# HGRN2 levels of 2 and 4 tokens, and of 8 and 16, computed as two groups of products

## The chip, the cores and the metric

The kernel runs on one core of one Trainium2 chip. The metric is the device time of one execution in microseconds, the median of three runs. TensorE (PE in the profile) does the matrix products, VectorE (DVE), ScalarE (ACT) and GpSimd (POOL) the rest, and SyncE (SP) issues the loads.

## The reference

Two layers of a block with three token mixers side by side (retention, HGRN2, differential attention) and a convolutional feed-forward part, for 16 meta tokens and 256 tokens of width 1024 in float32. What the change touches is the score matrix of HGRN2. For each of 8 heads of 128 features it is, between a query and an earlier key, the sum over features of query times key times the product of the forget gates between them:

```python
def step(state, xs):
    qc, kc, vc, lfc = xs
    cb = jnp.cumsum(lfc, axis=1)
    rel = cb[:, :, None] - cb[:, None, :]
    dec = jnp.where(causal, jnp.exp(jnp.where(causal, rel, 0.0)), 0.0)
    a = jnp.einsum('bqhd,bkhd,bqkhd->bhqk', qc, kc, dec)
    o = jnp.einsum('bhqk,bkhe->bqhe', a, vc) + jnp.einsum('bqhd,bhde->bqhe', qc * jnp.exp(cb), state)
```

The decay has a feature axis, so `a` is no single matrix product.

## The kernel before

**The main stream.** All weights are cut into 128x128 tiles, loaded in chunks of eight (`wraw`), split into a high half (`whi`, by ACT) and the rest (`wlo`, by DVE), and multiplied with the activations in three products each (lines 862 to 864, tile `main`). These products follow each other on TensorE from the first microsecond to the last; a pair of weight columns takes 48 of them, and `ORDER` (line 58) sets the order of the pairs. Everything else, the three mixers included, is put between them.

**The planner.** `_Plan` collects every operation with a cost, a due time (`key`) and its tiles, and writes out one fixed order for each engine. Names in `ORDER` that begin with `+`, `!` or `*` are marks: `+hgb` puts the scores of the second group of HGRN2 heads into the plan, and `!hgb` says by when they are due, since the due times of a part are spread up to the clock at its mark. All calls of ACT, DVE and small products go through one helper, line 549, so the profile gives them that line.

**The scores of HGRN2** (`hg_heads`, line 1010). It is called for two groups of four heads in each of two layers, four calls in all. The decay is split by reach: `LEVELS` are 1, 2, 4, 8, 16, 32 and 64. At reach s a token block of 2s has a left half of keys and a right half of queries. The keys `k` (`hf` in the profile) hold the decay up to the end of their half, the queries `q` (`hq`) that from the start of theirs, so one product gives the scores between the two halves. Afterwards the queries of the right half are multiplied by the total of the left half, the keys of the left half by the total of the right half, and the totals (`total`, tile `tot`) are multiplied in pairs.

For reach 1 to 16 the scores of four heads, two chunks and four blocks of 32 tokens are 32 small products (`quarters`, line 1057): the stationary side is the keys of one block of 32 tokens, the moving side the queries that are wanted, and four such products lie beside each other in four column strips of the array. The result is a bank `lev` of PSUM, from which masked copies (`fill`, line 1042, COPY_PREDICATED by DVE, with masks from `lev` of `masks`) write the wanted entries into `near`, 8 blocks of 32 columns. Reach 1 lists all 32 queries. Reach 2 lists 16 queries of its right halves and, from `odd` in the scratch tile `extra`, 16 odd queries that belong to reach 1. Reach 4, 8 and 16 list 16 queries each. Reach 32 and 64 (lines 1090 to 1122) go straight to the matrix `at`.

The 16 tokens behind the 256 (the tail) are handled by themselves: their keys and queries of each reach are copied by ACT into `kt` and `qt` (`qt1`, `qt2`, `qt4`, `qt8`), multiplied in two products `pm` and copied under masks into `am`. The products `px` (line 1163) connect the first chunk with the second one.

**Buffers.** `extra` has one of 14 slots of 4 times 272 columns. The gates (`hg`, `rg`, `m0`, `m1`, `m2`) have three buffers of 8 times 272 columns.

Of the kernel before, what the change touches and what calls it, by code (L numbers as in the profile page):

```python
# [13 lines left out]
U8 = mybir.dt.uint8  # L14
# [5 lines left out]
P = 128  # L20
# [3 lines left out]
T = META + SEQ  # L24
# [7 lines left out]
DA_DH = 64  # L32
MASKED = -1e30
LEVELS = (64, 32, 16, 8, 4, 2, 1)
TAIL = T - 2 * P
BANK = 512
CHUNK_TILES = 8
# [14 lines left out]
def _pairs(name, lo, hi):  # L52
    return [(name, j) for j in range(lo, hi)]
# [170 lines left out]
def _constants():  # L224
    f = np.float32
    c = np.zeros((P, C_END), f)
    c[:, C_COS_R : C_COS_R + T], c[:, C_SIN_R : C_SIN_R + T] = _rope_tables(RET_DK, 1)
    c[:, C_COS_D : C_COS_D + T], c[:, C_SIN_D : C_SIN_D + T] = _rope_tables(DA_DH, 2)
    k = np.arange(P)
    c[:, C_MASK + T - P : C_MASK + T] = np.where(k[None, :] <= k[:, None], 0.0, MASKED)  # L230
    c[:, C_IDENT : C_IDENT + P] = np.eye(P, dtype=f)
    lg = np.log1p(-np.exp2(-5.0 - np.arange(RET_HEADS, dtype=f))).astype(f)
    def decay(keys, queries):
        gap = (queries[None, :] - keys[:, None]).astype(f)
        d = np.exp(lg[None, :, None] * np.maximum(gap, 0)[:, None, :]) * f(RET_DK ** -0.5)
# [12 lines left out]
    c[:, C_FIRST:C_SUM] = np.where((hd == to) & (key <= q), 0.0, MASKED)  # L248
    c[:, C_SUM:C_MAP] = (hd == to) & (key == q)
    c[:, C_MAP:] = np.concatenate([m == 0, m == 1], axis=1)  # L250

    def level(s, keys, queries):
        q, key = np.arange(queries)[None, :], np.arange(keys)[:, None]
        return ((key // (2 * s) == q // s) & (key % (2 * s) < s)).astype(f)

    def odd(keys, queries):
# [7 lines left out]
    lev[:, :112] = np.tile(np.concatenate(block, axis=1), (4, 1))  # L266

    inner = [even(TAIL, 16), level(2, TAIL, 8), odd(TAIL, 8), level(4, TAIL, 8), level(8, TAIL, 8)]
    lev[:64, 2 * 64 :] = np.concatenate([np.kron(np.eye(4, dtype=f), x) for x in inner], axis=1)
    return c, dec, lev  # L270


# [335 lines left out]
def _trace(ctx, tc, plan, a, depth, probe):  # L608
# [41 lines left out]
    def bank(name):  # L650
        return new(bp, [P, 512], F32, "bank", 2, name)
# [4 lines left out]
    def tt(out, x, y, op):  # L656
        dve.tensor_tensor(out=out, in0=x, in1=y, op=op)
# [29 lines left out]
    masks = fixed([P, 5 * 64], "masks", U8)  # L687
    lev = masks[:, : 2 * 64]
    inner = masks[:64, 2 * 64 :]
    lev_f = slot("levf")[:, : 5 * 64]  # L690
    sync.dma_start(lev_f, a["lev"])
    plan.key = 18.0 + EARLY
    dve.tensor_copy(masks, lev_f)
# [243 lines left out]
    for li in range(depth):  # L937
# [72 lines left out]
        def hg_heads(b):  # L1010
# [28 lines left out]
            def right(t, s):  # L1039
                return halves(t, s, t.shape[2])[:, :, :, 1, :]  # L1040

            def fill(out, mask, x):

                s = out.shape[3]
                mask = mask.rearrange("p (n s) -> p n s", s=s).unsqueeze(1).to_broadcast([P, 8, 16 // s, s])
                dve.copy_predicated(out, mask, x.rearrange("p g (n s) -> p g n s", s=s))

            def blocks(calls, out, *moving):


# [15 lines left out]
            act.activation(odd[:, :, :, 64:], q[:, :, : 2 * P].rearrange("p h (c n two) -> p h c n two", c=2, two=2)[:, :, :, :, 1], AF.Copy)  # L1066
            tt(right(q, 1), right(q, 1), right(total, 1), MUL)
            room, at0 = slot("tot"), 0
            for i, s in reversed(list(enumerate(LEVELS))):

                pl = bank("lev")
                wide = pl[:, :256].rearrange("p (g t) -> p g t", g=8)
                some = pl[:, :128].rearrange("p (g t) -> p g t", g=8)
                tokens = lambda c, t: slice(c * P + 32 * t, c * P + 32 * t + 32)
                if s == 1:
                    quarters(wide, q, lambda hd, c, t: q[:, hd, tokens(c, t)])
                    dve.copy_predicated(near, lev[:, 80:112].unsqueeze(1).to_broadcast([P, 8, 32]), wide)
                elif s == 2:  # L1080
                    act.activation(odd[:, :, :, :64].rearrange("p h c (n s) -> p h c n s", s=2),
                                   q[:, :, : 2 * P].rearrange("p h (c n two s) -> p h c n two s", c=2, two=2, s=2)[:, :, :, :, 1, :], AF.Copy)
                    quarters(wide.rearrange("p g (two t) -> p g two t", two=2), odd,
                             lambda hd, c, t: odd[:, hd, c, :].rearrange("p (two t) -> p two t", two=2)[:, :, 16 * t : 16 * t + 16])
                    fill(right(near, 2), lev[:, 48:64], wide[:, :, :16])
                    fill(right(near, 1), lev[:, 64:80], wide[:, :, 16:])
                elif s < 32:
                    quarters(some.rearrange("p g (n s) -> p g n s", s=s), q, lambda hd, c, t: right(q[:, hd : hd + 1, tokens(c, t)], s)[:, 0])
                    fill(right(near, s), lev[:, 16 * (i - 2) : 16 * (i - 1)], some)
                elif s == 32:  # L1090
                    for t in range(4):
                        here = slice(32 * t, 32 * t + 32)
# [14 lines left out]
                else:  # L1107
# [15 lines left out]
                if s <= 8:  # L1123
                    act.activation(kt[:, 6 - i, :, :], k[:, :, tail], AF.Copy)
                    if s == 1:
                        act.activation(qt1, q[:, :, tail], AF.Copy)
                    else:
                        to = {2: qt2[:, :, :8], 4: qt4, 8: qt8}[s]
                        act.activation(to.rearrange("p h (n s) -> p h n s", s=s), right(q[:, :, tail], s), AF.Copy)

                end = 2 * P if s > 8 else T
                n = end // (2 * s)
                both = total[:, :, : 2 * n].rearrange("p h (n two) -> p h n two", two=2)
                first = both[:, :, :, 0:1]
# [6 lines left out]
                kl = halves(k, s, end)[:, :, :, 0, :]  # L1141
                tt(kl, kl, both[:, :, :, 1:2].to_broadcast([P, 4, n, s]), MUL)
                total = room[:, at0 : at0 + 4 * n].rearrange("p (h n) -> p h n", h=4)
                at0 += 4 * n
                tt(total.unsqueeze(3), first, both[:, :, :, 1:2], MUL)
# [426 lines left out]
```

## Time and profile before

| | before |
|---|---|
| time, median of 3 runs | 1330.01 us (1329.83 to 1330.66) |
| time of the profiled execution | 1330.22 us |
| its span, first to last instruction | 1328.4 us |
| granted TensorE clock | 0.999 |
| DMA, mean over the span | 164 GB/s |

The span is what the views of the profile cover; the time also holds what lies around it. In a row of a timeline the first number is the start in microseconds from the start of the span, the second the duration, then come engine, line, operation, output and inputs, shapes and count; rows that follow each other with the same text are merged. A duration overlaps the next instruction of the same engine, so what an instruction costs its engine is read from one start to the next. In the rows of `lev` the three numbers behind the colon are the least, median and greatest duration in nanoseconds. In rows by stretch each engine has its busy time and, in brackets, its instructions. A float32 product on TensorE stands as two records.

### The profile page before, as it was taken

The page shows a single profiled execution, that of the slowest core. Times are in us where ns is not written, and L with a number is a line of the kernel's source. Part 1 is how long each engine was busy: PE and PEld are TensorE (multiplying, and loading weights), DVE is VectorE, ACT ScalarE, POOL GpSimd, SP SyncE. Part 2 cuts the span into 40 slices and gives each one's busy share as a digit, 9 for nine tenths or more (in the row PEclk, how much of TensorE's full clock was granted, in tenths as well). Part 3 has the DMA queues.
Part 4 walks back from the last instruction along what each step waited for, and adds up shares of the span by engine and source line. Part 5 has one row for each costly group of instructions (what it writes and reads, how often), then busy time and mean ns, then how long its engine had stood idle before and what let it go on. Part 6 is the DMA issues. An engine that isn't in the chain of part 4 may idle for free.

```text
span 1328.4 us, 28916 instructions
## 1 busy us (share of the span) xinstructions
PE 1317.2 (99%) x11862; PEld 1288.8 (97%) x11862; DVE 962.0 (72%) x1630; ACT 813.3 (61%) x1372; POOL 83.6 (6%) x161
## 2 busy tenths in 40 slices
PE   9999999999999999999999999999999999999998
PEld 9999999999999999999999999999999999999986
DVE  7575777697576689886564757776985867898753
ACT  6747454746676567665446474557565775766643
POOL 5000000001010020000030000000011100200000
PEclk9999999999999999999999999999999999999999
DMA  7644543443544545555555445444445445465653
GB/s 270 193 142 153 167 161 128 143 143 128 179 139 159 175 159 175 182 170 187 177 173 179 158 157 163 160 136 144 141 153 175 141 160 198 138 208 189 199 184 109
DMA packets 60755, 219.07 MB, mean 165 GB/s; under 512 B 6864, under 2 KB 6992, under 8 KB 60624
## 3 DMA queue, kind: packets, MB, share of 16 engines
q1 hardware_dynamic: 60336, 216.71, 49.6%
q8 instruction: 93, 1.52, 0.5%
q10 hardware_dynamic: 288, 0.52, 0.1%
q14 instruction: 38, 0.31, 0.1%
HBM read 216.16 MB, written 1.05 MB: 164 GB/s over the span
## 4 chain that ended last, share of the span: by engine, by line
PE 94%; DVE 4%; issue 1%; ACT 0%; DMA 0%; SPq 0%; DVEq 0%
PE main L862 27%; PE main L864 27%; PE main L863 26%; PE fo L1372 2%; PE fo L1374 2%; PE fo L1373 2%; PE lev L1053 1%; DVE two_b L549 1%; PE ds L1237 1%; DVE wlo L549 1%; PE ms L549 1%; PE do L549 1%; PE ro L549 1%; PE ho L549 1%; PE vt L549 1%
## 5 line engine op out<-in xcount | busy, mean ns | idle before, releaser
L862 PE MATMUL main<-xh,whi 128*128 128x272 f32 (+1 forms) x2368 | 693.4, 293 | 0.3 <-issue 0.3
L864 PE MATMUL main<-xh,wlo 128*128 128x272 f32 (+1 forms) x2368 | 680.4, 287 | 0.7 <-DVE wlo L549 0.6
L863 PE MATMUL main<-xl,whi 128*128 128x272 f32 (+1 forms) x2368 | 671.7, 284 | 2.8 <-DVE xl L549 2.8
L549 DVE TENSOR_TENSOR wlo<-wraw,whi 128x1024 fp32r<-128x1024 f32 (+1 forms) x408 | 496.8, 1223 | 201.2 <-ACT whi L549 200.3
L549 ACT ACTIVATE whi<-wraw 128x1024 fp32r<-128x1024 f32 (+1 forms) x408 | 426.5, 1048 | 231.5 <-PE main L863 166.1
L863 PEld LDWEIGHTS main<-xl,whi 128*128 128x128 f32 x2368 | 448.9, 190 | 4.0 <-DVE xl L549 3.4
L862 PEld LDWEIGHTS main<-xh,whi 128*128 128x128 f32 x2368 | 445.6, 188 | 2.1 <-issue 0.4
L864 PEld LDWEIGHTS main<-xh,wlo 128*128 128x128 f32 x2368 | 444.6, 188 | 2.0 <-DVE wlo L549 2.0
L549 DVE SCALAR_TENSOR_TENSOR two_b<-main,small,two_b 128x256 f32<-128x256 f32 (+2 forms) x144 | 65.4, 487 | 29.1 <-ACT two_b L549 27.4
L549 ACT ACTIVATE two_b<-main,small 128x272 f32<-128x272 f32 (+1 forms) x72 | 37.3, 566 | 28.7 <-PE main L864 28.7
L549 POOL TENSOR_TENSOR y<-h,rstd 128x272 f32<-128x272 f32 x32 | 34.8, 1121 | 316.4 <-ACT rstd L549 316.4
L864 PE MATMUL main<-ghi,wlo 128*128 128x272 f32 x176 | 51.0, 290 | 0.0
L862 PE MATMUL main<-ghi,whi 128*128 128x272 f32 x176 | 50.9, 289 | 0.0
L863 PE MATMUL main<-glo,whi 128*128 128x272 f32 x176 | 50.2, 285 | 0.0
L549 ACT ACTIVATE vsrc<-main 128x544 f32<-128x544 f32 x24 | 15.0, 626 | 39.4 <-PE main L864 39.2
L862 PE MATMUL main<-b0hi,whi 128*128 128x272 f32 (+1 forms) x128 | 38.2, 298 | 0.0
L862 PE MATMUL main<-b1hi,whi 128*128 128x272 f32 (+1 forms) x128 | 38.1, 298 | 0.0
L864 PE MATMUL main<-yhi,wlo 128*128 128x272 f32 (+1 forms) x128 | 36.7, 286 | 0.0
L864 PE MATMUL main<-b2hi,wlo 128*128 128x272 f32 (+1 forms) x128 | 36.6, 286 | 0.0
L864 PE MATMUL main<-b1hi,wlo 128*128 128x272 f32 (+1 forms) x128 | 36.6, 286 | 0.0
L864 PE MATMUL main<-b0hi,wlo 128*128 128x272 f32 (+1 forms) x128 | 36.6, 286 | 0.0
L862 PE MATMUL main<-yhi,whi 128*128 128x272 f32 (+1 forms) x128 | 36.5, 285 | 0.0
(244 smaller groups left out, 1933.0 us busy)
## 6 DMA issues: line engine op xcount, KB each, us to landing
wraw<-in_w SPq DMA_DIRECT2D x402, 512.0 KB, 3.4
h<-in_h SPq DMA_DIRECT2D x4, 272.0 KB, 5.6
dec<-in_dec SPq DMA_DIRECT2D x2, 544.0 KB, 5.3
wraw<-in_w SPq DMA_DIRECT2D x4, 256.0 KB, 4.9
const<-in_const SPq DMA_DIRECT2D x1, 937.0 KB, 5.9
gain<-in_gl SPq DMA_DIRECT2D x1, 512.0 KB, 5.2
out<-y ACTq DMA_DIRECT2D x2, 256.0 KB, 2.8
out<-y SPq DMA_DIRECT2D x2, 256.0 KB, 2.7
```

Of the source, the lines that this page charges most:

```text
L549: self.plan.add(self.name, lambda: f(*args, **kw), cost, outs, ins, args[2] if method == "activation" else None)
L862: nc.tensor.matmul(o, wh, hi, start=first, stop=False)
L863: nc.tensor.matmul(o, wh, lo, start=False, stop=False)
L864: nc.tensor.matmul(o, wl, hi, start=False, stop=last)
L1053: nc.tensor.matmul(o, keys, x, start=True, stop=True)
L1237: nc.tensor.matmul(ss[m][:, at : at + nk], q[half, hd, q0 : q0 + P], k[half, hd, :nk], start=True, stop=True)
L1372: nc.tensor.matmul(o, gh, wh, start=False, stop=False)
L1373: nc.tensor.matmul(o, gl, wh, start=False, stop=False)
L1374: nc.tensor.matmul(o, gh, wl, start=False, stop=end)
```

## The change

Reach 2 and 4 become one group, reach 8 and 16 another. A block of four quarters of s tokens holds the halves of reach s and those of reach 2s. The queries of a block are listed once for each reach: quarters 1, 2 and 3 as they are; quarter 3 times the total of quarter 2, and quarter 2 times the total of quarter 1; quarter 3 times both. These six lists of s queries lie in `extra`, the last three made by DVE. For reach 2 the four odd queries of each block come in addition, so the moving side has 4 blocks of 16 columns, 64 in all; for reach 8 it has 48. `QUADS` says which quarter is written from which lists and which keys count for each. One call of `quarters` and three masked copies (four with the odd queries) then serve both reaches. The updates of queries, keys and totals for both reaches follow; the tail's queries of reach 4 are taken from the lists, in two copies. `extra` moves from the slots to the gate buffers, and the mark `!hgb` stands ahead of the pairs of `m0` instead of behind them.

```diff
+QUADS = ((1, ((1, 0), (2, 1), (3, 2))), (3, ((3, 1),)), (2, ((2, 0), (3, 0))))
...
-    + _pairs("dq", 0, 2) + _pairs("m0", 0, 4)
+    + _pairs("dq", 0, 2)
     + [("!hgb", 0)]
-    + _pairs("dv", 0, 2)
+    + _pairs("m0", 0, 4) + _pairs("dv", 0, 2)
...
-    lev = np.zeros((P, 2 * 64 + 192), f)
-    block = [level(s, 32, 16) for s in LEVELS[2:6]] + [odd(32, 16), even(32, 32)]
+    lev = np.zeros((P, 3 * 64 + 192), f)
+    block = [quads(2), quads(8), even(32, 32)]
...
-            extra = slot("extra")
-            odd = extra[:, : 8 * P].rearrange("p (h c t) -> p h c t", h=4, c=2)
+            extra = gate_tile("extra").rearrange("p k t -> p (k t)")
+            def quads(s):
+                width = 16 if s == 2 else 6 * s
+                n = (T if s == 2 else 2 * P) // (4 * s)
+                return extra[:, : 4 * n * width].rearrange("p (h n x) -> p h n x", h=4, n=n)
...
+                if s in (4, 16):
+                    continue
...
-                elif s == 2:
-                    act.activation(odd[:, :, :, :64].rearrange("p h c (n s) -> p h c n s", s=2),
-                                   q[:, :, : 2 * P].rearrange("p h (c n two s) -> p h c n two s", c=2, two=2, s=2)[:, :, :, :, 1, :], AF.Copy)
-                    quarters(wide.rearrange("p g (two t) -> p g two t", two=2), odd,
-                             lambda hd, c, t: odd[:, hd, c, :].rearrange("p (two t) -> p two t", two=2)[:, :, 16 * t : 16 * t + 16])
-                    fill(right(near, 2), lev[:, 48:64], wide[:, :, :16])
-                    fill(right(near, 1), lev[:, 64:80], wide[:, :, 16:])
-                elif s < 32:
-                    quarters(some.rearrange("p g (n s) -> p g n s", s=s), q, lambda hd, c, t: right(q[:, hd : hd + 1, tokens(c, t)], s)[:, 0])
-                    fill(right(near, s), lev[:, 16 * (i - 2) : 16 * (i - 1)], some)
+                elif s in (2, 8):
+                    x = quads(s)
...
+                    act.activation(x[:, :, :, : 3 * s], qs[:, :, :, s:], AF.Copy)
+                    tt(x[:, :, :, 3 * s : 4 * s], qs[:, :, :, 3 * s :], by(2), MUL)
+                    tt(x[:, :, :, 4 * s : 5 * s], qs[:, :, :, 2 * s : 3 * s], by(1), MUL)
+                    tt(x[:, :, :, 5 * s : 6 * s], x[:, :, :, 3 * s : 4 * s], by(1), MUL)
+                    each = 32 // (4 * s)
+                    wide = pl[:, : 8 * each * width]
+                    quarters(wide.rearrange("p (g t) -> p g t", g=8), extra,
+                             lambda hd, c, t: x[:, hd, (4 * c + t) * each : (4 * c + t + 1) * each, :].rearrange("p n x -> p (n x)"))
...
+                    for quarter, listed in QUADS:
+                        m = len(listed) * s
+                        dve.copy_predicated(to[:, :, :, quarter * s : quarter * s + m], mask[:, :, :, c : c + m], wide[:, :, :, c : c + m])
+                        c += m
+                    if s == 2:
+                        dve.copy_predicated(to.rearrange("p g n (k two) -> p g n k two", two=2)[:, :, :, :, 1], mask[:, :, :, 12:], wide[:, :, :, 12:])
...
+                    elif s == 4:
+                        to = qt4.rearrange("p h (n s) -> p h n s", s=4)
+                        act.activation(to[:, :, :, :2], qs[:, :, 2 * P // 8 :, 4:6], AF.Copy)
+                        act.activation(to[:, :, :, 2:], x[:, :, 2 * P // 8 :, 6:8], AF.Copy)
...
+                elif s in (2, 8):
+                    tt(qs[:, :, :, s : 2 * s], qs[:, :, :, s : 2 * s], by(0), MUL)
+                    tt(qs[:, :, :, 2 * s :], x[:, :, :, 4 * s : 6 * s], by(0, 2), MUL)
+                    if s == 8:
+                        qr = q[:, :, 2 * P + 8 : T]
+                        tt(qr, qr, total[:, :, 32:33].to_broadcast([P, 4, 8]), MUL)
...
+                if s in (2, 8):
+                    double(2 * s, T if s == 2 else 2 * P)
```

`double` is the former update of keys and totals for one reach, now a function of its own.

More of the change, by code (lines that the diff above doesn't have):

```diff
@@ L256, in level @@
         return ((key // (2 * s) == q // s) & (key % (2 * s) < s)).astype(f)
+    def quads(s):
+        key = np.arange(32)[:, None]
+        block = key // (4 * s)
+        out = []
+        for n in range(32 // (4 * s)):
+            for first, quarters in QUADS:
+                keys = np.repeat([to for _, to in quarters], s)[None, :]
+                out.append((block == n) & (key // s % 4 == keys))
+            if s == 2:
+                out.append(key == 8 * n + 1 + 2 * np.arange(4)[None, :])
+        return np.concatenate(out, axis=1).astype(f)
     def odd(keys, queries):
@@ L262, in even @@
         return (np.arange(keys)[:, None] == np.arange(queries)[None, :] // 2 * 2).astype(f)
-    lev = np.zeros((P, 2 * 64 + 192), f)
-    block = [level(s, 32, 16) for s in LEVELS[2:6]] + [odd(32, 16), even(32, 32)]
-    lev[:, :112] = np.tile(np.concatenate(block, axis=1), (4, 1))
+    lev = np.zeros((P, 3 * 64 + 192), f)
+    block = [quads(2), quads(8), even(32, 32)]
+    lev[:, :144] = np.tile(np.concatenate(block, axis=1), (4, 1))
     inner = [even(TAIL, 16), level(2, TAIL, 8), odd(TAIL, 8), level(4, TAIL, 8), level(8, TAIL, 8)]
-    lev[:64, 2 * 64 :] = np.concatenate([np.kron(np.eye(4, dtype=f), x) for x in inner], axis=1)
+    lev[:64, 3 * 64 :] = np.concatenate([np.kron(np.eye(4, dtype=f), x) for x in inner], axis=1)
     return c, dec, lev
@@ L686, in _trace @@
     ident = const[:, C_IDENT : C_IDENT + P]
[L687 to L690, printed above, removed]
+    masks = fixed([P, 6 * 64], "masks", U8)
+    lev = masks[:, : 3 * 64]
+    inner = masks[:64, 3 * 64 :]
+    lev_f = slot("levf")[:, : 6 * 64]
     sync.dma_start(lev_f, a["lev"])
@@ L1040, in right @@
                 return halves(t, s, t.shape[2])[:, :, :, 1, :]
[L1042 to L1046, printed above, removed]
             def blocks(calls, out, *moving):
@@ L1078, in hg_heads @@
                     quarters(wide, q, lambda hd, c, t: q[:, hd, tokens(c, t)])
-                    dve.copy_predicated(near, lev[:, 80:112].unsqueeze(1).to_broadcast([P, 8, 32]), wide)
-                elif s == 2:
-                    act.activation(odd[:, :, :, :64].rearrange("p h c (n s) -> p h c n s", s=2),
-                                   q[:, :, : 2 * P].rearrange("p h (c n two s) -> p h c n two s", c=2, two=2, s=2)[:, :, :, :, 1, :], AF.Copy)
-                    quarters(wide.rearrange("p g (two t) -> p g two t", two=2), odd,
-                             lambda hd, c, t: odd[:, hd, c, :].rearrange("p (two t) -> p two t", two=2)[:, :, 16 * t : 16 * t + 16])
-                    fill(right(near, 2), lev[:, 48:64], wide[:, :, :16])
-                    fill(right(near, 1), lev[:, 64:80], wide[:, :, 16:])
-                elif s < 32:
-                    quarters(some.rearrange("p g (n s) -> p g n s", s=s), q, lambda hd, c, t: right(q[:, hd : hd + 1, tokens(c, t)], s)[:, 0])
-                    fill(right(near, s), lev[:, 16 * (i - 2) : 16 * (i - 1)], some)
+                    dve.copy_predicated(near, lev[:, 112:144].unsqueeze(1).to_broadcast([P, 8, 32]), wide)
+                elif s in (2, 8):
+                    x = quads(s)
+                    count, width = x.shape[2:]
+                    qs = q[:, :, : count * 4 * s].rearrange("p h (n t) -> p h n t", n=count)
+                    gates = total[:, :, : 4 * count].rearrange("p h (n c) -> p h n c", c=4)
+                    by = lambda c, m=1: gates[:, :, :, c : c + 1].to_broadcast([P, 4, count, m * s])
+                    act.activation(x[:, :, :, : 3 * s], qs[:, :, :, s:], AF.Copy)
[6 more added lines that the diff above has]
+                             lambda hd, c, t: x[:, hd, (4 * c + t) * each : (4 * c + t + 1) * each, :].rearrange("p n x -> p (n x)"))
+                    wide = wide.rearrange("p (g n x) -> p g n x", g=8, n=each)
+                    to = near.rearrange("p g (n t) -> p g n t", n=each)
+                    m0 = 0 if s == 2 else 64
+                    mask = lev[:, m0 : m0 + each * width].rearrange("p (n x) -> p n x", n=each).unsqueeze(1).to_broadcast([P, 8, each, width])
+                    c = 0
+                    for quarter, listed in QUADS:
+                        m = len(listed) * s
+                        dve.copy_predicated(to[:, :, :, quarter * s : quarter * s + m], mask[:, :, :, c : c + m], wide[:, :, :, c : c + m])
+                        c += m
+                    if s == 2:
+                        dve.copy_predicated(to.rearrange("p g n (k two) -> p g n k two", two=2)[:, :, :, :, 1], mask[:, :, :, 12:], wide[:, :, :, 12:])
@@ L1126, in hg_heads, with double @@
                         act.activation(qt1, q[:, :, tail], AF.Copy)
+                    elif s == 4:
+                        to = qt4.rearrange("p h (n s) -> p h n s", s=4)
+                        act.activation(to[:, :, :, :2], qs[:, :, 2 * P // 8 :, 4:6], AF.Copy)
+                        act.activation(to[:, :, :, 2:], x[:, :, 2 * P // 8 :, 6:8], AF.Copy)
                     else:
-                        to = {2: qt2[:, :, :8], 4: qt4, 8: qt8}[s]
+                        to = {2: qt2[:, :, :8], 8: qt8}[s]
                         act.activation(to.rearrange("p h (n s) -> p h n s", s=s), right(q[:, :, tail], s), AF.Copy)
-                end = 2 * P if s > 8 else T
+                def double(s, end):
+                    nonlocal total, at0
+                    n = end // (2 * s)
+                    both = total[:, :, : 2 * n].rearrange("p h (n two) -> p h n two", two=2)
+                    kl = halves(k, s, end)[:, :, :, 0, :]
+                    tt(kl, kl, both[:, :, :, 1:2].to_broadcast([P, 4, n, s]), MUL)
+                    total = room[:, at0 : at0 + 4 * n].rearrange("p (h n) -> p h n", h=4)
+                    at0 += 4 * n
+                    tt(total.unsqueeze(3), both[:, :, :, 0:1], both[:, :, :, 1:2], MUL)
+                if s <= 8:
+                    tails(i, s)
+                if s == 2:
+                    parts = total
+                    double(2, T)
+                    tails(i - 1, 4)
+                    total, parts = parts, total
                 n = end // (2 * s)
-                both = total[:, :, : 2 * n].rearrange("p h (n two) -> p h n two", two=2)
-                first = both[:, :, :, 0:1]
+                first = total[:, :, : 2 * n].rearrange("p h (n two) -> p h n two", two=2)[:, :, :, 0:1]
                 if s == 1:
@@ L1140, in hg_heads @@
                     tt(qr, qr, first.to_broadcast([P, 4, n, s]), MUL)
[L1141 to L1145, printed above, removed]
+                if s == 2:
+                    total = parts
+                else:
+                    double(s, end)
+                if s in (2, 8):
+                    double(2 * s, T if s == 2 else 2 * P)
             pm = acc_bank("pm")
```

8 lines of the change are left out of this document (5 added, 3 removed).

## The prediction

> **What bounds the kernel now.** I read the page first, its span, its busy times and the chain of work that ended last.
>
> ```profile
> span 1328.4 us, 28916 instructions
> PE 1317.2 (99%) x11862; PEld 1288.8 (97%) x11862; DVE 962.0 (72%) x1630; ACT 813.3 (61%) x1372; POOL 83.6 (6%) x161
> PE 94%; DVE 4%; issue 1%; ACT 0%; DMA 0%; SPq 0%; DVEq 0%
> ```
>
> TensorE is busy all through and carries 94% of the chain. So what TensorE no longer has to do comes off the end, unless it must then wait. Next the tile into which the edited products write, `lev`, and busy time by engine in the four stretches that hold these products (two head groups in each of two layers).
>
> ```profile
> L1053 PE MATMUL lev<-hq,hf x1344: 179/186/243, 80.0 to 867.3; 128*32 128x16 f32 x116, 128*32 128x32 f32 x60, 128*32 128x64 f32 x16
> L1053 PE MATMUL lev<-extra,hf x320: 179/196/217, 86.5 to 867.3; 128*32 128x32 f32 x128, 128*32 128x16 f32 x32
> core 0: us, PE busy (x) PEld busy (x) DVE busy (x) ACT busy (x) POOL busy (x), PEclk, DMA share, GB/s
> 80.00:110.00 30.00, 30.00 (x612) 28.89 (x612) 22.86 (x38) 14.21 (x28) 0.71 (x4) 1.00 0.43 142
> 178.00:210.00 32.00, 31.72 (x625) 30.31 (x624) 25.61 (x45) 16.15 (x34) 0.68 (x3) 1.00 0.45 151
> 746.00:776.00 30.00, 30.00 (x621) 28.93 (x620) 23.18 (x38) 15.09 (x32) 0.79 (x5) 1.00 0.43 143
> 842.00:872.00 30.00, 30.00 (x616) 28.76 (x616) 24.46 (x45) 16.01 (x33) 0.77 (x4) 1.00 0.48 159
> ```
>
> 1344 and 320 records are 1664, 416 for each of four calls: five batches of 32 products (reaches 1, 2, 4, 8, 16), each product two records, then batches of 32 and 64 records (reaches 32 and 64). In these stretches TensorE has no idle time but 0.3 us, at full clock, while DVE has 6 to 7 us of 30 free and ACT 14 to 16.
>
> **The change, part by part.** *What TensorE loses.* A batch stands between main products, so its cost is what it adds to their steps. Three views of the timeline: reach 2 (32 columns), reach 4 (16 columns), reach 64 (half the records 64 columns wide, half 16).
>
> ```profile
> 86.28 0.28 PE L864 MATMUL main<-xh,wlo 128*128 128x272 f32 x1
> ...
> 86.50 0.76 PE L1053 MATMUL lev<-extra,hf 128*32 128x32 f32 x64
> ...
> 87.19 0.39 PE L862 MATMUL main<-xh,whi 128*128 128x272 f32 x1
> ...
> 87.54 0.29 PE L864 MATMUL main<-xh,wlo 128*128 128x272 f32 x1
> ...
> 88.66 0.29 PE L864 MATMUL main<-xh,wlo 128*128 128x272 f32 x1
> ...
> 89.04 0.29 PE L864 MATMUL main<-xh,wlo 128*128 128x272 f32 x1
> ...
> 89.25 0.74 PE L1053 MATMUL lev<-hq,hf 128*32 128x16 f32 x64
> ...
> 89.92 0.39 PE L862 MATMUL main<-xh,whi 128*128 128x272 f32 x1
> ...
> 90.27 0.29 PE L864 MATMUL main<-xh,wlo 128*128 128x272 f32 x1
> ...
> 103.27 0.29 PE L864 MATMUL main<-xh,wlo 128*128 128x272 f32 x1
> ...
> 103.48 0.32 PE L1053 MATMUL lev<-hq,hf 128*32 128x64 f32 x8
> ...
> 103.62 0.18 PE L1053 MATMUL lev<-extra,hf 128*32 128x16 f32 x2
> ...
> 103.66 0.32 PE L1053 MATMUL lev<-hq,hf 128*32 128x16 f32 x10
> ...
> 104.14 0.18 PE L1053 MATMUL lev<-extra,hf 128*32 128x16 f32 x2
> ...
> 104.19 0.19 PE L1053 MATMUL lev<-hq,hf 128*32 128x16 f32 x2
> ...
> 104.31 0.39 PE L862 MATMUL main<-xh,whi 128*128 128x272 f32 x1
> ```
>
> From 88.66 to 89.04 three main steps take 0.37 to 0.38 us, 0.124 each. From 89.04 to 90.27 there are three again and a batch: 1.23 less 0.37, so 16 columns cost 0.86. In the same way 32 columns cost 1.26 less 0.37, 0.89. Twice the columns add only 0.03, so up to there the count of records sets the price. Today reaches 2, 4, 8 and 16 cost 0.89 and three times 0.86, 3.47 us a call. After the change two batches of 64 records remain of these four, but 64 columns wide (four blocks of 16) and 48 wide.
>
> No batch of that width is in the trace, so I bound it. The lower end: the reach-64 batch takes 0.83 from its first record to the next main product (103.48 to 104.31) against 0.67 with 16 columns (89.25 to 89.92); 32 wide records add 0.16, so 64 add 0.32, and the batch costs 1.18. The upper end looks inside that batch. The same point of a head returns at 103.62 and, three heads on, at 104.14, so a head takes 0.173. Of its sixteen records the eight narrow ones start 0.007 apart (six of them between 103.62 and 103.66), 0.055 in all, which leaves 0.118 for eight wide ones. Sixty-four of these are 0.94, and the step from the last to the next main product (104.19 to 104.31) 0.12: 1.06 against the 0.69 of 32 columns, so 0.89 and 0.37 are 1.26. I take 1.25, since the second way separates the widths. By columns, 48 take three quarters of 0.94, 0.71, and 0.12: 0.83 against 0.67, which gives 1.02; the floor is 0.86, were the width hidden; I take 1.04. Together 2.29 (2.04 to 2.30). **A call saves 1.18 us, four calls 4.7** (1.17 to 1.43 each, 4.7 to 5.7).
>
> The Trainium skill speaks of this width in TensorEngine Tiling (Array Packing), section Performance Considerations (Instruction Overhead): a product has a fixed cost of some 60 cycles, so that one column takes as long as 60. By that rule 48 and 64 columns would cost little more than 16, and the gain would be near 6.9. The trace agrees between 16 and 32 columns (0.86 and 0.89) but not at 64 (0.118 for eight records against 0.055).
>
> *What DVE and ACT get.* DVE's queue holds nine more instructions a call: three products with totals for each group (272 and 256 elements), one more masked copy for each, a small one for the tail; the updates of `q` shrink (544 and 544 become 272 and 544; 544 and 512 become 256, 512 and 32).
>
> ```profile
> 182.58 0.68 ACT L549 ACTIVATE extra<-hq 128x512 f32<-128x512 f32 x1
> ...
> 183.94 0.72 DVE L549 TENSOR_TENSOR hq<-hq,tot 128x544 f32<-128x544 f32 x1
> ...
> 184.57 0.17 DVE L549 TENSOR_TENSOR tot<-tot 128x16 f32<-128x16 f32 x1
> 184.66 1.22 DVE L549 TENSOR_TENSOR wlo<-wraw,whi 128x1024 fp32r<-128x1024 f32 x1
> ...
> 185.79 0.93 DVE L549 COPY_PREDICATED near<-masks,lev 128x128 f32<-128x128 uint8 x2
> ...
> 188.06 0.74 PE L1053 MATMUL lev<-hq,hf 128*32 128x16 f32 x64
> ...
> 188.85 0.30 DVE L549 COPY_PREDICATED near<-masks,lev 128x128 f32<-128x128 uint8 x1 [1.57 <-PE lev L1053]
> 189.05 0.72 DVE L549 TENSOR_TENSOR hq<-hq,tot 128x544 f32<-128x544 f32 x1
> ```
>
> By steps from start to start, 544 elements take 0.63 (183.94 to 184.57) and 16 take 0.09, so 272 or 256 take 0.35 or 0.33. A masked copy costs from 0.20 (188.85 to 189.05) to 0.46 (half of the pair's 0.93, whose runs are of two and one elements). So the products are 1.05 and 1.0, the copies about 0.5 and 0.3, the updates give back 0.5: some 2.3 us of DVE a call. ACT gets one copy of 816 elements in place of 512, one of 768 and one small one more, some 1.3 us by the 0.68 of the row. All this lies under main products: DVE goes from 22.9 to 25 of 30 us in the first stretch. Without that cover it would cost 9 us over four calls.
>
> The cover can fail at two places, because a batch is queued on TensorE ahead of main products, and what it lacks holds them all. Before the 64-wide batch the three products (1.05) come in, and the instruction order of the changed program sets the batch 15 main products later than reach 2 stood, 1.9 us. Before the 48-wide batch, group b has, after the 64-wide one, four masked copies (0.8 to 1.8), two updates of `hf` (1.27 by the 0.63), three products (1.0) and one of `q` (0.33): 3.4 to 4.4. DVE starts 0.79 after the batch (188.06 to 188.85), and 0.38 later for the width: done 4.6 to 5.6 after its start. In that order 36 main products stand between, 4.5 us, and the batch itself 1.25: 5.7, and four transposes besides. Group a has 42. So I count no wait, with bounds of 0 and 0.3 at each of eight batches, 2.4 in all.
>
> Four things I set at nothing. The moved mark makes group b due four weight pairs sooner: in the changed order its last batch stands 15 main products earlier, and its products of tail tokens, with their masked copies, stand ahead of the retention work instead of among it; the instructions are the same and the queue of DMAs is not touched. The halves of the weights on DVE stand at least 38 main products ahead of their use in that order (40 before), 4.7 us, and cover any delay of 2.3. The scratch tile now takes a third buffer among the gates: its last reader in group b stands about 100 main products before `m0` is evacuated into it. The larger mask is 64 columns more in one load and one copy ahead of the first batch, 0.07 us by the DVE steps, while TensorE runs on.
>
> The sum: the profiled execution took 1330.22 us, 1.8 around its span of 1328.4, and the median is 1330.01. Less 4.7: span 1323.7, time 1325.5, and **1325.3 by the median**.
>
> **The rivals.** *Waits take the place of the removed batches*: masked copies all at 0.46 and the order closer than counted; six to eight waits of 0.3 to 0.5 give back about 3, 1328.3. For it: the margin before the 48-wide batch can be as small as 0.1. Against: no batch waits now; in the three views the first record follows the main product before it by 0.21 to 0.22 alike. A wait here would also hold the masked copies behind the batch, and so the next update of `hf` and the next batch.
>
> *Slower: the new forms on DVE.* The copies now go in runs of six, two and four, and the products in blocks with a broadcast total. If a copy took 0.95 and a product 0.7, the four and three between the two batches would need 5.9 instead of 2.9 or less; TensorE would stand 3 us in each call, 12 less 4.7: 1337. It decides for slower from 4.8 us on (2.9, and a quarter of 4.7 plus 2.7). Against: updates of `q` in runs of two with a broadcast total run at the 0.63 of the row, and the worst copy is 0.46. The Trainium skill, TensorEngine Tiling (Array Packing), section Performance Considerations (PSUM Bottleneck), warns that tiling speeds up the products and not the copies out of PSUM, which is this rival; the row at 185.79 bears out that such copies can be dear, not that they bind.
>
> *Width is free*: both batches at 0.87, 8 times 0.87, 6.9 less: 1323.1. Against it stands the reach-64 batch, which costs more than one of 16 columns. The Trainium skill's TensorEngine Tiling (Array Packing), section Performance Considerations (Instruction Overhead), is for it.
>
> *The gain is lost in the feed*: DVE and ACT late with weights, 1329.5. Against: 5 us of DVE still free in the stretch.
>
> **How the numbers follow.** Forecast 0.78; waits 0.09; slower 0.04; width free 0.06; feed 0.03. The range reaches from near the free width to the waits, 1323.6 to 1328.3, and leaves out the slower case, the feed and the edges. About 0.2%, 2.7 us, is what can be told from no change; faster than 1327.3 are the forecast, the free width and a third of the waits, 0.87; the rest of the waits and the feed are 0.09; slower 0.04.
>
> **What would show it.** In the profile after: 1152 records on `lev` in place of 1664; a 64-wide batch that adds about 1.25 us between main products and a 48-wide one about 1.04; no idle time of TensorE before either; DVE up by some 9 us, ACT by 5. It is wrong if the start of these batches lies far behind the main product before them (a wait), or if the wide records start much farther apart than 0.015.

## The result, and the profile after

| | before | after |
|---|---|---|
| median, same chip, 5 runs each | 1329.83 us (1329.74 to 1330.66) | 1324.66 us (1324.02 to 1324.83) |
| ratio after / before | | 0.9958, 95% interval 0.9947 to 0.9969 |
| profiled span | 1328.4 us | 1323.0 us |

The ratio is 0.42% below one. The medians differ by 5.2 us (0.39%), the profiled spans by 5.4; the forecast was 4.7. The page of the changed kernel, its span, its busy times and the chain of work that ended last:

```profile
span 1323.0 us, 27904 instructions
PE 1311.0 (99%) x11350; PEld 1284.1 (97%) x11350; DVE 971.6 (73%) x1666; ACT 818.6 (62%) x1380; POOL 83.7 (6%) x161
PE 93%; DVE 4%; DMA 1%; issue 1%; ACT 0%; SPq 0%; DVEq 0%; ACTq 0%
```

TensorE is still what bounds the kernel: 99% busy, 93% of the chain. It has 512 records fewer and 6.2 us less busy time; DVE has 9.6 us more and ACT 5.3 more, and neither shows in the span. The instructions on `lev`, and the masked copies out of it:

```profile
L1062 PE MATMUL lev<-hq,hf x576: 179/196/243, 79.6 to 862.1; 128*32 128x32 f32 x128, 128*32 128x64 f32 x48, 128*32 128x16 f32 x16
L1062 PE MATMUL lev<-extra,hf x576: 179/206/244, 88.0 to 862.1; 128*32 128x64 f32 x88, 128*32 128x48 f32 x84, 128*32 128x16 f32 x20
L564 DVE COPY_PREDICATED near<-masks,lev x32: 229/336/454, 82.6 to 854.5; 128x128 f32<-128x128 uint8 x12, 128x192 f32<-128x192 uint8 x8, 128x64 f32<-128x64 uint8 x8, 128x256 f32<-128x256 uint8 x4
```

576 and 576 are 1152 records, as forecast. The same four stretches as before, busy time by engine (the columns are those of the header row shown with the stretches of before):

```profile
80.00:110.00 30.00, 30.00 (x473) 29.14 (x462) 24.97 (x47) 16.73 (x34) 0.71 (x4) 1.00 0.45 147
178.00:210.00 32.00, 32.00 (x452) 31.08 (x452) 29.68 (x58) 18.41 (x38) 0.89 (x3) 1.00 0.46 155
746.00:776.00 30.00, 30.00 (x446) 29.21 (x445) 23.83 (x47) 18.22 (x37) 0.79 (x5) 1.00 0.43 135
842.00:872.00 30.00, 30.00 (x440) 29.07 (x439) 27.86 (x58) 17.23 (x36) 0.77 (x3) 1.00 0.51 165
```

TensorE is busy from end to end in all four, at full clock. DVE has gone up by 2.1 in the first stretch; in the second and fourth, by 4.1 and 3.4, part of it the tail work that the moved mark brings into these stretches. It still has 2 to 6 us of 30 free. Now the two new batches in the timeline of TensorE. The columns are start, duration, engine, line, operation, tiles, shape and count:

```profile
87.76 0.29 PE L879 MATMUL main<-xh,wlo 128*128 128x272 f32 x1
87.98 1.10 PE L1062 MATMUL lev<-extra,hf 128*32 128x64 f32 x64
89.01 0.39 PE L877 MATMUL main<-xh,whi 128*128 128x272 f32 x1
...
89.36 0.29 PE L879 MATMUL main<-xh,wlo 128*128 128x272 f32 x1
...
94.22 0.29 PE L879 MATMUL main<-xh,wlo 128*128 128x272 f32 x1
94.44 0.89 PE L1062 MATMUL lev<-extra,hf 128*32 128x48 f32 x64
95.26 0.39 PE L877 MATMUL main<-xh,whi 128*128 128x272 f32 x1
...
95.62 0.29 PE L879 MATMUL main<-xh,wlo 128*128 128x272 f32 x1
...
190.54 0.29 PE L879 MATMUL main<-xh,wlo 128*128 128x272 f32 x1
190.76 0.89 PE L1062 MATMUL lev<-extra,hf 128*32 128x48 f32 x64
```

Read as before: from 87.76 to 89.36 are 1.60 us, less three main steps (0.37) 1.23: the 64-wide batch. From 94.22 to 95.62 are 1.40, less 0.37: 1.03, the 48-wide one (1.02 unrounded). In all four calls the step from the last main product before the batch to the first one behind it is 1.25 for the 64-wide and 1.02 to 1.04 for the 48-wide batch. Each first record follows the main product before it by 0.22 (87.76 to 87.98, 94.22 to 94.44, 190.54 to 190.76), which is what a batch without a wait had before.

Where the 5.4 us lie is seen by lining up the two traces at the same main product, counted from the start of the program. Between these points lie the four head groups that the change touches:

| main product | before starts, us | after starts, us | after is ahead by | gained since the row above |
|---|---|---|---|---|
| 240 | 39.42 | 39.03 | 0.39 | 0.39 (start of the program) |
| 720 | 106.65 | 105.03 | 1.62 | 1.23 (group a, layer 0) |
| 1560 | 232.97 | 229.73 | 3.24 | 1.62 (group b, layer 0) |
| 5520 | 764.55 | 760.13 | 4.42 | 1.18 (group a, layer 1) |
| 6360 | 887.04 | 881.37 | 5.67 | 1.25 (group b, layer 1) |

Three of the groups give 1.18 to 1.25, the batches' own 3.47 less 2.25, 1.22. The second gives 0.4 more, for in the trace of before TensorE stands still there once, behind the batch of reach 4 at 188.06, which the trace after doesn't have:

```profile
189.07 0.39 PE L862 MATMUL main<-xh,whi 128*128 128x272 f32 x1 [0.28 <-issue]
```

In brackets is the idle time, and "issue" says that the profile shows nothing that TensorE waited for. With what lies around it the gap costs 0.33: the kernel moved, below, has the same products between these two rows and takes 0.33 less without a gap. Behind the last row the lead goes back from 5.67 to the 5.4 of the spans. So some 4.9 us are the batches, and 0.4 at the start, 0.3 at the gap and some 0.25 lost again behind the last row are differences between two executions that none of the edits is shown to cause.

### The profile page after: what moved, and what is told of

The parts are those of the page before. It is cut to its first block, busy times and chain, and to the rows that moved or that the text cites. A ratio compares the mean times of both kernels' runs of the same rounds, so it can differ in the third digit from the quotient of the medians.

```text
span 1323.0 us, 27904 instructions
## 1 busy us (share of the span) xinstructions
PE 1311.0 (99%) x11350; PEld 1284.1 (97%) x11350; DVE 971.6 (73%) x1666; ACT 818.6 (62%) x1380; POOL 83.7 (6%) x161
## 4 chain that ended last, share of the span: by engine, by line
PE 93%; DVE 4%; DMA 1%; issue 1%; ACT 0%; SPq 0%; DVEq 0%; ACTq 0%
PE main L877 27%; PE main L879 27%; PE main L878 26%; PE fo L1438 2%; PE fo L1440 2%; PE fo L1439 2%; DVE two_b L564 1%; DVE wlo L564 1%; PE lev L1062 1%; PE ds L1303 1%; PE do L564 1%; PE ms L564 1%; DMA wraw<-in_w 1%; PE ro L564 1%; PE ho L564 1%
## 5 line engine op out<-in xcount | busy, mean ns | idle before, releaser
L564 POOL COPY tails<-vsrc 128x32 f32<-128x32 f32 x32 | 10.0, 329 | 418.2 <-ACT vsrc L564 365.9
```

What stands on the lines that cost most here:

```text
L564: self.plan.add(self.name, lambda: f(*args, **kw), cost, outs, ins, args[2] if method == "activation" else None)
```

## The experiments

Theory: time is saved where TensorE issues fewer records, a batch costs what its records take to stream, and everything else is hidden. Each kernel ran beside the kernel before on one chip; ratios are to it. A span also holds a start that differs between executions: in the ten traces main product 240 starts at 38.60 to 40.01 us. So where the text says "on the common stretch", it is the time from main product 240 to 6360, the first and the last row of the table above, which all ten traces have: 847.62 us before, 842.34 after, 5.28 less. The first four are parts of the change (before: 1330.33 us, 26 runs).

**moved**: the kernel before, with only the two edits beside the products.

```diff
-    + _pairs("dq", 0, 2) + _pairs("m0", 0, 4)
+    + _pairs("dq", 0, 2)
...
-    + _pairs("dv", 0, 2)
+    + _pairs("m0", 0, 4) + _pairs("dv", 0, 2)
...
-            extra = slot("extra")
+            extra = gate_tile("extra").rearrange("p k t -> p (k t)")
```

> The kernel before with the two side edits alone: the mark of the second head group ahead of the pairs of m0, and the scratch tile in a gate buffer; no grouped products. Theory (the gain is TensorE's smaller work on the tile lev): 1664 records stay, so no change, ratio 1.000, within 0.7 us. Rival (a part of the gain is the new order or the buffers): 1 to 2 us faster, ratio near 0.999, with the costs of the batches unchanged.

Measured: 1329.7 us (11 runs), ratio 0.9995 (0.9986 to 1.0004), span 1327.7, still 1664 records on `lev`. No gain that can be told from none. On the common stretch it takes 847.32, 0.31 less than before, as much as the gap of before. The order of the work and the buffers alone don't make the 5 us.

**only2** and **only8**: one of the two groups of products alone, with the side edits.

```diff
# only2
-                if s in (4, 16):
+                if s in (4,):
...
-                elif s in (2, 8):
+                elif s in (2,):
# only8
-                if s in (4, 16):
+                if s in (16,):
...
-                elif s in (2, 8):
+                elif s in (8,):
...
```

The masks, copies and updates of the other two reaches, not shown here, are those of before.

> The changed kernel with reach 8 and 16 as before and reach 2 and 4 grouped. Theory: per call the batches of 0.89 and 0.86 us become one of 1.23 (the 64-wide batch in the trace of the changed kernel), 0.52 less, four calls 2.1 us, ratio 0.9984. Rival (width free): 0.88 less per call, 3.5 us. Rival (gain from order): below 1 us.

> The changed kernel with reach 2 and 4 as before and reach 8 and 16 grouped. Theory: per call two batches of 0.86 become one of 1.02, 0.70 less, four calls 2.8 us, ratio 0.9979; with the other group alone it adds up to the 4.9 of both. Rival (the groups share a gain that needs both): the two sum to well under 4.9.

Measured: only2 1327.83 us (11 runs), ratio 0.9983 (0.9974 to 0.9992), span 1326.3; only8 1326.8 us (10 runs), ratio 0.9974 (0.9965 to 0.9984), span 1324.7. That is 0.17% and 0.26%, together 0.43%, as much as the whole change has (0.42%). So the two add up, and the second group is the larger, in the order of their terms (0.89 and 0.86 less 1.23 is 0.52 a call, 2.1 in all; twice 0.86 less 1.02 is 0.70, 2.8). By the medians both came out some tenths above these terms, 2.5 and 3.5, but the intervals are 2.4 us wide. The traces show the terms themselves: on the common stretch only2 takes 845.23 and only8 844.47, 2.40 and 3.15 less than before, and without the 0.33 of the gap of before 2.07 and 2.82.

**mark_back**: the changed kernel, with the mark of group b behind `m0` again.

```diff
-    + _pairs("dq", 0, 2)
+    + _pairs("dq", 0, 2) + _pairs("m0", 0, 4)
...
-    + _pairs("m0", 0, 4) + _pairs("dv", 0, 2)
+    + _pairs("dv", 0, 2)
```

> The changed kernel with the mark of the second head group behind the pairs of m0 again, the scratch tile still in a gate buffer. Theory: the mark frees nothing that TensorE waits for, so the time is that of the changed kernel within 0.7 us, ratio to before near 0.996. Rival: the third gate buffer comes free too late, m0's evacuation holds TensorE, and 1 us or more of the gain is lost in idle time after main products of m0.

Measured: 1325.46 us (5 runs), ratio 0.9964 (0.9951 to 0.9976), span 1323.6 against 1323.0, on the common stretch 842.64 against 842.34. The mark neither earns nor costs anything that these runs resolve, and in this trace TensorE has no idle time of 0.1 us between 37 and 345 and between 503 and 1153, so the gate buffer doesn't hold it in `m0`. The mark was rightly set at nothing.

The other four ask what a batch costs and how thin its cover is (before: 1330.33 us, 19 runs).

**twice**: the two grouped batches issued twice over.

```diff
-                    for o, keys, x in calls:
-                        nc.tensor.matmul(o, keys, x, start=True, stop=True)
+                    for _ in range(2 if again else 1):
+                        for o, keys, x in calls:
+                            nc.tensor.matmul(o, keys, x, start=True, stop=True)
...
```

`again` is set for the two grouped batches alone.

> The changed kernel with each of the two grouped batches issued twice into the same bank (the result is the same). Theory (TensorE's work sets the end one to one): 2 times 2.25 us less the entry saved, 8 batches of 0.93 to 1.1 more each, 7.9 to 8.9 us over the changed kernel, so 3 to 4 us over the kernel before, ratio 1.002 to 1.003. Rival (time on TensorE around these batches is partly slack): less than 6 us over the changed kernel.

Measured: 1332.13 us (10 runs), ratio 1.0013 (1.0004 to 1.0023), span 1330.8, 7.8 over the changed kernel's 1323.0 (7.0 by the medians, each against the kernel before beside it). That is under what was expected: the added streaming arrives at the end, but it is less than was added on paper. TensorE's timeline of this kernel shows why:

```profile
87.98 0.29 PE L879 MATMUL main<-xh,wlo 128*128 128x272 f32 x1
88.20 1.99 PE L1063 MATMUL lev<-extra,hf 128*32 128x64 f32 x128
...
90.48 0.29 PE L879 MATMUL main<-xh,wlo 128*128 128x272 f32 x1
...
189.93 0.28 PE L879 MATMUL main<-xh,wlo 128*128 128x272 f32 x1 [0.32 <-issue]
...
193.96 1.23 PE L1063 MATMUL lev<-extra,hf 128*32 128x48 f32 x96
195.64 0.55 PE L1063 MATMUL lev<-extra,hf 128*32 128x48 f32 x32 [0.45 <-issue]
```

From 87.98 to 90.48 less 0.37 are 2.13 for 128 records of 64 columns, 0.90 more than for 64. So a record takes 0.014 us, and of the batch's 1.23 some 0.34 is the way in and out of it, paid once. The 48-wide batch goes from 1.02 to 1.70, 0.0106 a record, and again 0.34 is left. Four calls at 0.90 and 0.68 are 6.3. On the common stretch it takes 849.85, 7.51 over the changed kernel: three of the four groups are 1.58 to 1.60 longer, as the two batches are, and the second is 2.74 longer. In that one TensorE stands still twice with nothing to wait for, 0.32 at 189.93 and 0.45 inside the 48-wide batch at 195.64, with what lies around them 1.16. Another 0.2 lies at the start. The expectation took too little off for the way in and out. The rival, in which the batches lie in free time of TensorE, falls.

**wide8**: the 48-wide batch padded to 64 columns, by 16 that nothing reads.

```diff
...
+                        quarters(pl.rearrange("p (g t) -> p g t", g=8), extra,
+                                 lambda hd, c, t: extra[:, ((hd * 2 + c) * 4 + t) * 48 : ((hd * 2 + c) * 4 + t) * 48 + 64])
+                        wide = pl.rearrange("p (g t) -> p g t", g=8)[:, :, :48]
...
```

> The changed kernel with the batch of reach 8 at 64 columns in place of 48; the 16 more are results that nothing reads. Theory (price by columns): the batch adds 1.23 us between main products instead of 1.02, as that of reach 2 does. Rival (a fixed price up to some 60 columns): 1.02 stays, and the extra of reach 2 comes from its blocks of 16.

Measured: 1325.38 us (1 run), span 1323.6. One time settles nothing at this size; the price of the batch does, in TensorE's timeline of this kernel:

```profile
93.88 0.29 PE L879 MATMUL main<-xh,wlo 128*128 128x272 f32 x1
94.10 1.10 PE L1062 MATMUL lev<-extra,hf 128*32 128x64 f32 x64
...
95.48 0.29 PE L879 MATMUL main<-xh,wlo 128*128 128x272 f32 x1
```

1.60 less 0.37 is 1.23 in place of 1.02, to the hundredth the price of reach 2's batch. Nothing but the columns has changed, so the columns are what is paid for; a price by the count of records falls. It arrives at the end, too: on the common stretch this kernel takes 0.91 more than the changed one, and four times 0.21 are 0.84. With 0.34 taken off, a record takes 0.0081 us at 16 columns, 0.0086 at 32, 0.0106 at 48 and 0.0139 at 64. That the narrow batches have the same way in and out is assumed: only the two wide ones were doubled. The last two are 0.22 ns a column, and the floor of the first two is reached at some 38 columns (an estimate from these four). The Trainium skill, TensorEngine Tiling (Array Packing), section Performance Considerations (Instruction Overhead), puts the end of that floor at about 60 columns. It names no element type; for the float32 products of this case, each of two records in four strips, the floor ends well below, so the measurement decides.

**late2** and **late6**: one DVE product that the 48-wide batch needs is issued two and six times more, the planner being told of one.

```diff
-                    tt(x[:, :, :, 5 * s : 6 * s], x[:, :, :, 3 * s : 4 * s], by(1), MUL)
+                    late = lambda o=x[:, :, :, 5 * s : 6 * s], a=x[:, :, :, 3 * s : 4 * s], g=by(1), n=2 if s == 8 else 0: [
+                        nc.vector.tensor_tensor(out=o, in0=a, in1=g, op=MUL) for _ in range(1 + n)]
...
```

> The changed kernel with the third product of the second group issued three times on DVE in place of once, 0.67 us more that the planner is not told of, so the order of all engines stays. In the trace of the changed kernel the last update of keys ends 0.76 to 0.91 us before the 48-wide batch. Theory (that margin is cover): no wait at that batch, at most 0.3 at the reach-32 batch behind it; the time of the changed kernel within 1 us. Rival (no margin, DVE sets these batches): 0.67 at each of four, 2.7 us more.

> The same with the product issued seven times, 2.0 us more on DVE unknown to the planner. Theory: the margin of 0.76 to 0.91 is used up and TensorE waits 1.1 to 1.3 us at each of four 48-wide batches, 4.4 to 5.2 us over the changed kernel, about the time of the kernel before. Rival (DVE off the path altogether): no change.

Measured: late2 1327.19 us (10 runs), ratio 0.9975 (0.9966 to 0.9985), span 1325.5, 2.5 over the changed kernel (2.0 by the medians). That is nearer the rival's expectation than the theory's. late6 1336.49 us (4 runs), ratio 1.0044 (1.0029 to 1.0059), span 1334.4, 11.4 over: the right sign, but more than twice the size expected. First late2, DVE's own row, and then the two next batches on TensorE:

```profile
189.25 1.34 DVE L1110 TENSOR_TENSOR extra<-extra,tot 128x256 f32<-128x256 f32 x3
```

```profile
191.27 0.29 PE L879 MATMUL main<-xh,wlo 128*128 128x272 f32 x1
191.70 0.89 PE L1062 MATMUL lev<-extra,hf 128*32 128x48 f32 x64
```

```profile
99.12 0.29 PE L879 MATMUL main<-xh,wlo 128*128 128x272 f32 x1
99.75 0.46 PE L1062 MATMUL lev<-hq,hf 128*32 128x32 f32 x32 [0.34 <-DVE hf L564]
```

Three of the same product take 1.34, so the two repeats cost 0.46 each, not the 0.33 of the expectation, and the delay is 0.92. At the 48-wide batch only 0.21 of it appears: its first record follows by 0.43 in place of 0.22 (191.27 to 191.70). The margin took the other 0.7. Not all of the 0.86 there could be used: the waiting batch starts 0.15 behind the end of its update (0.05 in group a). So far the theory nearly holds. But the batch of reach 32, 5 us behind the 48-wide one, now waits too: in group a, the last of the rows above, it starts 0.63 behind the main product in place of 0.22 (99.12 to 99.75), for the update of `hf`. DVE was still late. In this call it works without a pause from the update ahead of the first of these batches to the one ahead of the second (93.97 to 99.70), so it makes up next to nothing of its 0.9, while TensorE had been held by 0.21 alone. Over the four calls the waits are 0.08 to 0.22 at the 48-wide batches and 0.16 to 0.58 at those of reach 32, 2.1 together. The expectation counted the first place alone.

Now late6, TensorE's timeline, and busy time in stretches of 2 us around two of its four long waits:

```profile
94.78 0.29 PE L879 MATMUL main<-xh,wlo 128*128 128x272 f32 x1
97.05 1.51 PE L1062 MATMUL lev<-extra,hf 128*32 128x48 f32 x64 [1.99 <-DVE hf L564]
98.49 0.60 PE L877 MATMUL main<-xh,whi 128*128 128x272 f32 x1
```

```profile
94.00:96.00 2.00, 1.06 (x9) 0.85 (x7) 1.86 (x5) 0.92 (x1) 0.00 (x0) 1.00 0.00 0
96.00:98.00 2.00, 0.95 (x48) 0.95 (x52) 2.00 (x5) 0.26 (x1) 0.00 (x0) 0.75 0.00 0
98.00:100.00 2.00, 2.00 (x35) 1.88 (x28) 1.57 (x3) 0.00 (x0) 0.00 (x0) 0.50 0.30 51
100.00:102.00 2.00, 2.00 (x16) 2.00 (x16) 1.83 (x7) 0.24 (x1) 0.00 (x0) 0.89 0.77 254
...
195.00:197.00 2.00, 0.06 (x5) 0.09 (x9) 1.97 (x5) 0.17 (x1) 0.00 (x0) 1.00 0.07 26
197.00:199.00 2.00, 2.00 (x74) 1.94 (x75) 2.00 (x4) 0.08 (x1) 0.00 (x0) 1.00 0.05 12
```

Six repeats make DVE 2.75 late (steps of 0.45 to 0.46). The waits at the 48-wide batches are 1.9 to 2.06 (94.78 to 97.05 less the usual 0.22), 8.1 over the four calls, and those at reach 32 come to 0.9. Behind the first of the long waits the granted clock, the column after POOL, goes to 0.75 and 0.50 before it comes back: the 48-wide batch takes 1.51 in place of 0.89 and the next main product 0.60 in place of 0.39, some 1.5 us in all. Behind the wait at 195 it stays at 1.00. These three make 10.5 of the 11.4; 0.5 more lies at the start of this execution.

## Why the prediction was right

*What bounds the kernel.* TensorE does, and it was shown from both sides: with 512 records fewer the end comes 5.4 earlier, and with those 512 added again (twice) it comes 7.8 later than that, neither of them eaten by free time.

*The batches.* 1.25 and 1.04 were taken, and 1.23 and 1.02 measured, so a call saves 1.22 in place of 1.18, 4.9 in place of 4.7. Of the two ways to read the width out of the reach-64 batch, the one that separated wide records from narrow ones was the nearer; it gave 0.0148 for a record of 64 columns, against 0.0139. The forecast stood at the low end of its own 4.7 to 5.7. That the whole came out half a microsecond above it is mostly chance: the start and the gap, which no sum over the edits could have had.

*DVE and ACT.* 9 and 5 were forecast, and 9.6 and 5.3 measured. Both were hidden.

*The cover.* DVE's timeline between the two batches of group b, layer 0, where the margin was counted as smallest (the 64-wide batch starts at 184.61):

```profile
185.78 1.60 DVE L564 COPY_PREDICATED near<-masks,lev 128x192 f32<-128x192 uint8 x4
187.18 0.76 DVE L564 TENSOR_TENSOR hf<-hf,tot 128x544 f32<-128x544 f32 x1
187.85 0.74 DVE L564 TENSOR_TENSOR extra<-hq,tot 128x256 f32<-128x256 f32 x2
188.51 0.42 DVE L564 TENSOR_TENSOR extra<-extra,tot 128x256 f32<-128x256 f32 x1
188.85 0.42 DVE L564 TENSOR_TENSOR hq<-hq,tot 128x256 f32<-128x256 f32 x1
189.18 0.72 DVE L564 TENSOR_TENSOR hf<-hf,tot 128x544 f32<-128x544 f32 x1
```

The four masked copies take 1.40 by their steps (185.78 to 187.18), the first update of `hf` 0.67, the three products 1.00, `q` 0.33, and the second update ends at 189.90: 4.1, inside the 3.4 to 4.4, and 5.3 after the batch's start, inside the 4.6 to 5.6. The 48-wide batch starts at 190.76, so the margin is 0.86. Counted were 0.1 to 1.1, and in the four calls it is 0.76 to 0.91, least in group a of layer 0, for which the prediction had counted more main products. At the other place, ahead of the 64-wide batch, the last product of its lists ends 0.89 to 1.45 before the batch. What the prediction didn't count is the margin behind that, ahead of reach 32: 0.32 to 0.68 there, the smaller of the two.

*Set at nothing.* The mark and the gate buffer without the products (moved), and the mark taken back with them (mark_back), move nothing that can be told. The larger mask is written at 40.1, in 0.36 us in place of 0.32, and the stretch from main product 240 to 480 takes 29.93 us in both traces. The halves of the weights weren't tried apart; TensorE has no idle time in the four stretches that they could have caused.

*The rivals.* Width free: refuted, by 1.23 against 1.02 in wide8. Lost in the feed: refuted, TensorE is busy for all of the four stretches and waits for no weights there. Waits and the slower kernel didn't come, but they were real: with 0.92 us more of DVE in front of one batch a call, about two fifths of the gain is gone (2.5 of 5.4 by the spans, 2.0 of 5.2 by the medians), and with 2.75 the kernel is slower than before by 0.44%. The prediction let the slower case decide from 4.8 us of copies and products between the batches; in group b they take 2.4 here, 3.3 in late2 and 5.2 in late6. A straight line between the ratios of these two puts 0.2% slower at 4.5 us and break-even at 4.0 (an estimate: between them nothing was run). The place was right, and the price a little low, since the lateness is paid at two batches and, once, with the clock.

## What to carry to other kernels

On a TensorE that never waits, a batch of small float32 products costs a fixed way in and out (0.34 us here) and then its records, and a record costs nearly the same up to some 38 columns (the estimate above) and goes by columns from there: merge batches that are narrower, and count the columns that merging adds when it goes beyond. Price the merged width from the widest records in the trace, kept apart from the narrow ones beside them. Work that moves to a free engine is hidden by the margin ahead of the next batch that needs it, 0.3 to 0.9 us here, of which 0.05 to 0.15 can't be used, and not the several microseconds that a busy share leaves free; and lateness that one batch doesn't absorb is handed on to the next.

## What was not expected of the hardware

The same product, issued again onto the same elements, takes 0.46 us a step on DVE (1.34 for three), where products onto different elements step by 0.33 to 0.34 (188.51 to 188.85, 188.85 to 189.18). Both read the same shapes; why wasn't tried.

A wait of 2.06 us on TensorE was followed by a granted clock of 0.50, and the three others of 1.9 to 2.06 in the same execution were not. The Trainium skill, TensorE: Matmul & The Clock Gate, section Part 1: The HAM clock gate, puts the fall to half clock behind at least one idle window of about 3.4 us. In this trace a shorter wait was enough, once in four.

TensorE stood still once in the kernel before (0.28 us) and two times in the kernel twice (0.32 and 0.45) with nothing in the profile to wait for, all three between 189 and 196 us, in the same head group; the cause is open. At the size of this change, 5 us, such gaps and a start that differs by up to 1.4 between executions are no small part of what is measured; one profile's span doesn't carry a smaller claim, and times taken between the same two instructions of two traces do better.
